# A hybrid state-space and convolution layer: the latent convolution's buffers get rows of 8 KB, and the out-projection's second tile is prepared earlier

## The chip, the cores and the metric

The kernel runs on one core of a Trainium2 chip. The metric is the device time of one execution in microseconds. Before the change it is 1872.1 us, the median of three runs (1870.85 to 1872.3).

## What is computed

One layer over 256 context tokens and 2048 latent tokens (a grid of 32 rows by 64 columns), with a model width of 1024. All tokens are normalised and modulated, and go through one input projection. Its columns feed two branches, whose outputs meet in one output projection. Cut to what matters:

```python
h = rms_norm(x, g_pre) * (1 + scale) + shift
u = h @ w_in
z, xbc, dt_raw, ga, gb, gsil = jnp.split(u, [...], axis=-1)
y_ssd, h_fin = ssd_branch(z, xbc, dt_raw, ...)        # a scan in both directions, gated by silu(z)
c = depthwise_conv(ga * sigmoid(gb), conv_w, conv_b)  # 31 taps along the rows of the grid, per channel
y_conf = silu(layer_norm(c, ln_g, ln_b)) * silu(gsil)
out = jnp.concatenate([y_ssd, y_conf], axis=-1) @ w_out
y = x + gate * rms_norm(out, g_post)
```

For the context the convolution runs along its 256 tokens; for the latent it runs along the 32 grid rows, separately for each of the 64 columns and 1024 channels.

## The kernel before, in words

**Tiling.** The tokens are 18 tiles of 128: tiles 0 and 1 are context, 2 to 17 latent. For the input projection they are grouped in five blocks: block 0 is the context (256 tokens), blocks 1 to 4 are 512 latent tokens each. Channels are handled in groups of 128, numbered j = 0 to 7. Float32 products are made from three matmuls on split operands (high x high, low x high, high x low; lines 391 to 393), so each weight has a high half `wh` and a low half `wl`.

**Phases.** Half 0 projects blocks 1, 2 and 0, half 1 blocks 3 and 4. In each half come the scan's columns (`xp`), then eight `gab_unit`s (the convolution's gated input; matmuls `gb` and `ga`, line 391), then silu units for z and for the gate gsil (`silu_unit`; matmuls `sp`). These units are interleaved with the scan (`px`, `py`, `po`, and its DMAs `yp<-yg`, `st<-sb`), with the context's convolution on DVE (`cg`, line 608), and in half 1 with `lat_conv`, the latent's. `SLOT` says which of the buffers of normalised input each block takes.

**The convolution's path.** `gab_unit` stores its result (`gth`) for channel group j and one block to the DRAM buffer `GL[j]` (line 556): 128 channels, for each one a row of 512 tokens, 2 KB. The latent convolution wants grid rows on the partitions, since the taps run along them. So `lat_load` (line 629) reads `GL[j]` back transposed, into `cx`: four DMAs, each 32 rows x 32 channels x 64 columns, in pieces of 64 columns, 256 B. It also loads the taps (`kd`, line 628). `lat_conv` multiplies 32 x 32 tap matrices with the columns (`cp`, line 648), adds the bias into `cvv` (line 652), and stores it to `CV` (line 657), again in four DMAs of 1024 pieces of 256 B, so that `CV` is channel-major over tokens. Last, `conf_load` (line 1098) reads one tile of 128 tokens, all channels, in 1024 pieces of 512 B.

**Queues.** SP issues nearly all DMAs, one after the other: a DMA whose buffer or data isn't ready holds all behind it, weight loads (`wh<-whd`, `wl<-wld`, lines 359 and 360) among them. A scheduler that keeps a timeline of its own fixes the order on each engine.

**The transition.** The out-projection works tile by tile in the order 17, 16, ..., 0. For a tile it takes the scan's output `y` (with state products `qo`, gate by `z`, sum of squares `zr`), scales it by a norm and splits it into `yh` and `yl`; and the convolution's output `cn` (centred by the mean `cm`, squared into `v`, summed into `nq`, scaled, silu, gated by `gsl`), split into `ph` and `pl`. `norms` sums `zr` and `nq` over the partitions by matmul (`pm`), takes roots on DVE and POOL (`yms`, `yr`), and `spread` hands them to all partitions by matmul (`pn`). The matmuls `op` then multiply both with the out-projection's weights, 16 pairs `woh` and `wol`. `load_wo` (lines 969 to 976) makes a pair: a DMA to a staging tile `wst`, a cast on ACT, a subtraction on DVE. Staging has two buffers in turn. Weights 9 to 15 are loaded only when the last silu unit is done, since their pool takes over memory of that phase. While that goes on, before prepares tile 17's end and tile 16's whole input.

**Line 77.** In the loop, DVE, ACT and PE run through the wrapper `InOrder`: with `on` set, each instruction is kept behind the one that the program issued before it on that engine, so the scheduler can't move it ahead. What was issued before `on` was set, it may still order freely among itself. Loop instructions appear as line 77 in the profile, whichever helper records them.

The wrapper and the loop's head:

```python
        f = getattr(self._eng, name)
        if not self.on:
            return f
        return lambda *a, **k: self._tc.keep_in_program_order(f(*a, **k))
...
    V.on = S.on = T.on = True
    for a, i in enumerate(order):
        banks(i)
        pt = hl(p2, "p", 1, i, v)
        out_part(pso[i], yh, 0, 1)
        rs = None if last else norms(nxt, yz, nq)
```

Of the kernel before, what the change touches and what calls it, by code (L numbers as in the profile page):

```python
# [17 lines left out]
P = 128  # L18
D = 1024
KT = D // P  # L20
# [7 lines left out]
TOK = (0, 256, 768, 1280, 1792)  # L28
BNS = (256, 512, 512, 512, 512)
ORDER = ((1, 2, 0), (3, 4))  # L30
SLOT = (0, 1, 2, 1, 2)
RAWO = (2, 260, 772, 130, 642)
NF = 3
PREP = 16
# [27 lines left out]
def take(gen, n):  # L62
    for _ in range(n):
        yield next(gen, None)
# [16 lines left out]
def backbone_kernel(ctx, tc, xa, xt_in, cols, rows, wconv, conf_b, gp_row, bg_row, state0, w_mod, w_dt, w_in, w_out,  # L81
# [12 lines left out]
    def dram(name, shape):  # L94
        return drp.tile(shape, F32, tag=name, name=name)
# [1 line left out]
    XB = [dram(f"xb{h}", [NCT * P, n]) for h, n in ((0, N1), (1, N2))]  # L97
    HALO = dram("halo", [NCT, P, 130])
    ZS = [dram(f"zs{h}", [D, HT[h] * P]) for h in range(2)]
    GL = [dram(f"gl{j}", [P, NT * P]) for j in range(KT)]  # L100
    GS = [dram(f"gs{h}", [D, HT[h] * P]) for h in range(2)]
    CV = dram("cv", [D, NT * P])
    YP = [dram(f"yp{i}", [P, D]) for i in range(NT)]
    ST = [dram(f"st{i}", [P, D]) for i in range(NT)]
    LT = [dram(f"lt{h}", [HT[h] * 32, P]) for h in range(2)]
# [437 lines left out]
    def gab_unit(half, j, hb):  # L543
        wb = next_w()
        wa = next_w()
        gl_done.discard(j)
        for b in ORDER[half]:
            BN, o = BNS[b], TOK[b]
            pg = bank("mm", f"gb{half}_{j}_{b}")
            yield from mm_cm(pg, wb, hb[b])  # L550
            th = ev(f"gth{half}_{j}_{b}")[:, :BN]
            S.activation(th, pg[:, :BN], AF.Tanh, scale=0.5)
            pa_ = bank("mm", f"ga{half}_{j}_{b}")
            yield from mm_cm(pa_, wa, hb[b])
            V.scalar_tensor_tensor(th, th, 1.0, pa_[:, :BN], ADD, MUL)  # L555
            DMA.dma_start(GL[j][:, o:o + BN], th)
        if half:
            gl_done.add(j)

    def silu_unit(half, c0, dst, j, hb, order=None):  # L560
        w = next_w()
        for b in order or ORDER[half]:
            BN, o = BNS[b], TOK[b] - half * HT[0] * P
            ps = bank("mm", f"sp{half}_{c0}_{j}_{b}")
            yield from mm_cm(ps, w, hb[b])
            th = ev(f"sth{half}_{c0}_{j}_{b}")[:, :BN]
            S.activation(th, ps[:, :BN], AF.Tanh, scale=0.5)  # L567
            V.scalar_tensor_tensor(th, th, 1.0, ps[:, :BN], ADD, MUL)  # L568
            DMA.dma_start(dst[half][j * P:(j + 1) * P, o:o + BN], th)
# [28 lines left out]
    def ctx_conv(j, tile):  # L598
        g = tile(f"cg{j}")
        G.memset(g[:, 0:15], 0.0)  # L600
        G.memset(g[:, 271:286], 0.0)
        DMA.dma_start(g[:, 15:271], GL[j][:, 0:256])
        yield
        acc = g[:, 512:768]
        w0 = C_CONFW + j * CW
        V.tensor_scalar(acc, g[:, 0:256], cv[:, w0:w0 + 1], cfb2[:, j:j + 1], MUL, ADD)
        for t in range(1, CW):
            V.scalar_tensor_tensor(acc, g[:, t:t + 256], cv[:, w0 + t:w0 + t + 1], acc, MUL, ADD)  # L608
            if t % 3 == 0:
                yield  # L610
        o = g[:, 768:1024]
        S.mul(o, acc, 0.5)
        DMA.dma_start(CV[j * P:(j + 1) * P, 0:256], o)
        yield


# [4 lines left out]
    def lat_load(j, lp):  # L621
        kd = lp.tile([P, 32, 32], F32, tag="kd", name=f"kd{j}", bufs=2)
        x = lp.tile([P, 32, 64], F32, tag="cx", name=f"cx{j}", bufs=2)
        lat_in[j] = kd, x
        for a in range(4):
            rs = slice(a * 32, (a + 1) * 32)
            src = bass.AP(tensor=wconv.tensor, offset=(j * 4 + a) * 64 * 32, ap=[[32, 32], [1, 1024]])
            DMA.dma_start(kd[rs].rearrange("p r g -> p (r g)"), src)
            DMA.dma_start(x[rs], GL[j][:, 256:].rearrange("(g a) (r w) -> a r g w", a=4, w=64)[a])

    def lat_conv(j, lp, cbb, more):
        if j not in lat_in:
            lat_load(j, lp)
        kd, x = lat_in.pop(j)
        yield
        kt = lp.tile([P, 32, 32], F32, tag="kt", name=f"kt{j}", bufs=1)
        S.copy(kt[:, :, ::-1].rearrange("p g r -> p r g"), kd)
        if more(j + 1):
            lat_load(j + 1, lp)
        yield  # L640
        vt = lp.tile([P, 32, 64], F32, tag="cvv", name=f"cvv{j}", bufs=1)
        for h in range(2):
            ps = {a: bank("ss", f"cp{j}_{a}") for a in (2 * h, 2 * h + 1)}
            for q in range(8):
                for u in range(4):
                    for a in ps:
                        rs = slice(a * 32, (a + 1) * 32)
                        T.matmul(ps[a][u * 32:(u + 1) * 32, q * 64:(q + 1) * 64], kt[rs, u * 8 + q, :], x[rs, u * 8 + q, :],
                                 start=True, stop=True)
            yield  # L650
            for a in ps:
                V.scalar_tensor_tensor(vt[:, a::4, :], ps[a].rearrange("p (c w) -> p c w", w=64), 0.5,
                                       cbb[:, j, a::4].unsqueeze(2).to_broadcast([P, 8, 64]), MUL, ADD)
            yield
        for u in range(4):
            c0 = j * P + u * 32
            DMA.dma_start(CV[c0:c0 + 32, 256:].rearrange("c (r w) -> r c w", w=64), vt[u * 32:(u + 1) * 32])


    def pass_a(i):  # L660
# [217 lines left out]
    def run(gen):  # L878
        for _ in gen:
            pass  # L880
# [36 lines left out]
    xbc_phase(0, first, hb, [hprep(2, hb), hprep(0, hb)], tails, dt_post(0))  # L917
    extra = chain([gate_rows()] + [ctx_conv(j, big) for j in range(4)])
    interleave(post(0, 6), merge(scan(range(9)), 68, extra, 9 + 4 * 13), 90 * 8)
    last = [silu_unit(0, GS0, GS, j, hb, (1, 2, 0)) for j in (6, 7)]  # L920
    prep = hprep(3, hb)
    s = 0
    for b in range(3):
# [99 lines left out]
    def state_add(i):  # L1023
        for g in range(2):
            sg = sl[i]["st"][:, g * 512:(g + 1) * 512]
            if i == NCTX - 1:
                V.tensor_copy(Sb[g], sg)
            else:
                V.tensor_tensor(Sb[g], Sb[g], sg, ADD)
# [49 lines left out]
    def lo(t):  # L1079
        V.tensor_tensor(t[1], t[2], t[0].bitcast(F32), SUB)  # L1080
# [14 lines left out]

    def conf_load(i):
        n = p2.tile([P, 8, P], F32, tag="cn", name=f"cn{i}", bufs=2)
        DMA.dma_start(n, CV[:, i * P:(i + 1) * P].rearrange("(c p) t -> p c t", p=P))
        return n

    def conf_sum(i, n):
        v = p2.tile([P, 8, P], F32, tag="v", name=f"v{i}", bufs=2)
        return v, sum8(v[:, 0, :], v[:, 0:4, :], n)

    def conf_mean(i, t):
        mean = bank("ss", f"cm{i}")[:, 0:P]
        T.matmul(mean, ones, t, start=True, stop=True)
        return mean

    def conf_centre(n, mean):  # L1110
        V.scalar_tensor_tensor(n, rows8(mean), -1.0 / D, n, MUL, ADD)

    def conf_square(v, n):
        S.activation(v, n, AF.Square)
        return v

    def conf_sqsum(i, v):
        return v, sum8(p2.tile([P, P], F32, tag="nq", name=f"nq{i}", bufs=1), v[:, 0:4, :], v)

    def gs_load(i):  # L1120
        gs = p2.tile([P, 8, P], F32, tag="gs", name=f"gsl{i}", bufs=1)
        DMA.dma_start(gs, chan_slice(GS, i))
        return gs

    def conf_scale(n, pb):
        V.tensor_tensor(n, n, rows8(pb[:, P:2 * P]), MUL)
# [63 lines left out]
    for g in range(2):  # L1190
        state_decay(i, g)
    state_add(i)
    run(take(blocks, 5))
    for k in range(6, 9):
        load_wo(k, wo2)
        run(take(blocks, 8))
    run(blocks)
    last = [silu_unit(1, GS0, GS, j, hb) for j in range(5, 8)]
    for b in range(2):
        for m, u in enumerate(last):  # L1200
            run(take(u, 8))
            if b == 0 and m == 1:
                rs = norms(i, yz, None)
            if b == 1 and m == 0:
                ssd_scale(i, yz[0], spread(i, rs))
                yh = hl(p0, "y", 2, i, yz[0])
                lo(yh)
                ph_b[1].close()
                p2 = ph_1.enter_context(tc.tile_pool(name="p2", bufs=1))
                n = conf_load(i)  # L1210
                v, t = conf_sum(i, n)
                conf_centre(n, conf_mean(i, t))
    for u in last:
        run(u)
    v, nq = conf_sqsum(i, conf_square(v, n))
    conf_scale(n, spread(i, norms(i, None, (v, nq))))
    gs = gs_load(i)
    conf_silu(n, v)
    conf_gate(v, gs)
    ph_b[2].close()  # L1220
    ph_h.close()
    p3 = ph_1.enter_context(tc.tile_pool(name="p3", bufs=1))
# [1 line left out]
    for k in range(9, 16):  # L1224
        load_wo(k, wo4)
    load_gg(0)
    i = order[1]
    ssd_load(i)
    st_load(i)
    n = conf_load(i)  # L1230
    state_mm(i)
    y_state(i)
    y_gate(i)
    yz = y_sum(i)
    for g in range(2):
        state_decay(i, g)
    v2, t = conf_sum(i, n)
    conf_centre(n, conf_mean(i, t))
    nq = conf_sqsum(i, conf_square(v2, n))
    gs = gs_load(i)  # L1240
    ssd_load(order[2])
    n2 = conf_load(order[2])
    V.on = S.on = T.on = True
# [133 lines left out]
```

## Time and profile before

| what | value |
|---|---|
| median of three runs | 1872.1 us |
| the profiled execution | 1872.28 us |
| its span in the trace | 1870.5 us |
| mean granted TensorE clock | 0.984 |
| PE, DVE, ACT busy | 97%, 64%, 46% |
| DMA moved | 375.22 MB, mean 201 GB/s |
| half-0 gab units, roughly | 230 to 560 us |
| half-1 gab units and latent convolution, roughly | 930 to 1230 us |
| last silu units end | 1405 us |
| out-projection loop | to the end |

How to read it: engine names are PE (matmul), PEld (its weight loads), DVE, ACT, POOL and SP (its queue as SPq). `out<-in` gives an instruction's output and input by the program's names. A bracket at the end of a timeline's row is the idle time ahead of that instruction and what ended it. In the table of windows each row is one stretch: its length, then busy time and count for PE, PEld, DVE, ACT and POOL, then the granted PE clock as a share of full speed, the DMA engines' busy share and GB/s.

### The profile page before, as it was taken

How to read it: one execution, taken by the hardware profiler on the slowest of the kernel's cores; microseconds unless marked ns; L12 is line 12 of the kernel's file. 1: busy time of each engine (PE TensorE's matmuls, PEld its weight loads, DVE VectorE, ACT ScalarE, POOL GpSimd, SP SyncE). 2: the span in 40 equal slices, each digit the busy share in tenths (PEclk: the TensorE clock that was granted, in tenths of full speed). 3: DMA queues.
4: the chain of work that ended last, by engine and by line, in shares of the span. 5: the costliest groups of instructions: out<-in, count | busy, mean ns of one | idle time of the engine just before them, and what ended most of it. 6: DMA issues, size and time to landing. Idle time of an engine off the chain costs nothing.

```text
span 1870.5 us, 30012 instructions
## 1 busy us (share of the span) xinstructions
PE 1808.1 (97%) x11223; PEld 1493.1 (80%) x11223; DVE 1203.1 (64%) x1841; ACT 863.8 (46%) x1956; POOL 175.9 (9%) x281
## 2 busy tenths in 40 slices
PE   7899999999999999999998989999997999999998
PEld 4788887788888888888876767777886888888887
DVE  2477887785555553577587845666347777777773
ACT  3646424455445441644224545553326454444441
POOL 0002001111101100100001111110000111111110
PEclk9899999999999999999999999999998999999999
DMA  8656575576566654545589798895967656666632
GB/s 298 219 199 210 203 241 181 175 254 219 195 217 211 226 196 169 167 155 189 170 200 233 199 251 229 258 244 175 331 189 209 183 167 174 172 171 178 182 106 79
DMA packets 305309, 375.22 MB, mean 201 GB/s; under 512 B 85254, under 2 KB 204678, under 8 KB 305164
## 3 DMA queue, kind: packets, MB, share of 16 engines
q1 hardware_dynamic: 284428, 335.56, 58.1%
q10 hardware_dynamic: 20736, 37.76, 7.1%
q8 instruction: 88, 1.44, 0.3%
q14 instruction: 57, 0.47, 0.1%
HBM read 243.66 MB, written 129.59 MB: 200 GB/s over the span
## 4 chain that ended last, share of the span: by engine, by line
PE 85%; DMA 7%; DVE 4%; ACT 1%; issue 1%; SPq 1%; POOL 0%; POOLq 0%; DVEq 0%; ACTq 0%
PE op L77 21%; PE sp L391 7%; PE sp L392 7%; PE sp L393 7%; PE xp L391 5%; PE xp L392 5%; PE xp L393 5%; PE ga L391 3%; PE ga L393 2%; PE ga L392 2%; PE gb L391 2%; PE gb L393 2%; PE gb L392 2%; DMA lb<-lt 2%; PE py L732 2%; DVE cg L608 2%
## 5 line engine op out<-in xcount | busy, mean ns | idle before, releaser
L696 ACT ACTIVATE lb<-lb,WB 128x128 f32<-128x128 f32 x576 | 184.3, 391 | 167.7 <-POOL lb L688 162.1
L391 PE MATMUL sp<-hh,wh 128*128 128x512 f32 (+1 forms) x640 | 238.5, 373 | 0.0
L392 PE MATMUL sp<-hl,wh 128*128 128x512 f32 (+1 forms) x640 | 236.0, 369 | 0.0
L393 PE MATMUL sp<-hh,wl 128*128 128x512 f32 (+1 forms) x640 | 235.8, 368 | 0.0
L391 PE MATMUL xp<-hh,wh 128*128 128x512 f32 (+1 forms) x480 | 179.3, 375 | 6.1 <-ACT wh L366 4.9
L688 POOL TENSOR_SCALAR_AFFINE_SELECT lb<-lb 128x512 f32<-128x512 f32 x144 | 112.6, 786 | 714.2 <-ACT el L685 366.7
L393 PE MATMUL xp<-hh,wl 128*128 128x512 f32 (+1 forms) x480 | 179.0, 373 | 0.0
L392 PE MATMUL xp<-hl,wh 128*128 128x512 f32 (+1 forms) x480 | 178.9, 373 | 0.0
L488 DVE SCALAR_TENSOR_TENSOR cva<-raw,cwh,cva 128x1280 f32<-128x1280 f32 (+1 forms) x96 | 142.1, 1488 | 19.7 <-ACT cva L482 17.9
L391 PEld LDWEIGHTS sp<-hh,wh 128*128 128x128 f32 x640 | 120.6, 189 | 20.8 <-DVE sth L568 0.4
L393 PEld LDWEIGHTS sp<-hh,wl 128*128 128x128 f32 x640 | 120.6, 188 | 20.7
L392 PEld LDWEIGHTS sp<-hl,wh 128*128 128x128 f32 x640 | 120.7, 189 | 19.8
L391 PE MATMUL ga<-hh,wh 128*128 128x512 f32 (+1 forms) x320 | 122.0, 381 | 6.8 <-DMA wh<-whd 6.3
L391 PE MATMUL gb<-hh,wh 128*128 128x512 f32 (+1 forms) x320 | 121.4, 379 | 5.3 <-DVE gth L555 5.3
L393 PE MATMUL ga<-hh,wl 128*128 128x512 f32 (+1 forms) x320 | 119.4, 373 | 0.5 <-DMA wl<-wld 0.5
L392 PE MATMUL gb<-hl,wh 128*128 128x512 f32 (+1 forms) x320 | 119.6, 374 | 0.0
L393 PE MATMUL gb<-hh,wl 128*128 128x512 f32 (+1 forms) x320 | 119.6, 374 | 0.0
L392 PE MATMUL ga<-hl,wh 128*128 128x512 f32 (+1 forms) x320 | 119.2, 373 | 0.0
L568 DVE SCALAR_TENSOR_TENSOR sth<-sth,sp 128x512 f32<-128x512 f32 (+1 forms) x80 | 50.4, 630 | 97.3 <-ACT sth L567 96.9
L391 PEld LDWEIGHTS xp<-hh,wh 128*128 128x128 f32 x480 | 92.1, 192 | 23.2 <-ACT wh L366 5.5
L608 DVE SCALAR_TENSOR_TENSOR cg<-cg,cv 128x256 f32<-128x256 f32 x240 | 107.6, 487 | 0.6
L392 PEld LDWEIGHTS xp<-hl,wh 128*128 128x128 f32 x480 | 91.7, 191 | 15.7 <-DVE hl L312 0.4
(252 smaller groups left out, 3745.8 us busy)
## 6 DMA issues: line engine op xcount, KB each, us to landing
lb<-lt ACTq DMA_DIRECT2D x144, 256.0 KB, 4.5
wr<-in_w_in SPq DMA_DIRECT2D x88, 256.0 KB, 4.7
whd<-wh SPq DMA_DIRECT2D x44, 512.0 KB, 3.6
wld<-wl SPq DMA_DIRECT2D x44, 512.0 KB, 5.2
wh<-whd SPq DMA_DIRECT2D x44, 512.0 KB, 4.6
wl<-wld SPq DMA_DIRECT2D x44, 512.0 KB, 5.8
xT<-xb SPq DMA_DIRECT2D x18, 512.0 KB, 5.0
yp<-yg SPq DMA_DIRECT2D x36, 256.0 KB, 4.3
```

Of the source, the lines that this page charges most:

```text
L77: return lambda *a, **k: self._tc.keep_in_program_order(f(*a, **k))
L391: T.matmul(ps[:, :BN], wh[:, k, :], hh[:, k, :], start=(k == 0), stop=False)
L392: T.matmul(ps[:, :BN], wh[:, k, :], hl[:, k, :], start=False, stop=False)
L393: T.matmul(ps[:, :BN], wl[:, k, :], hh[:, k, :], start=False, stop=(k == KT - 1))
L488: V.scalar_tensor_tensor(a[:, :n], raw[:, t:t + n], cwh[:, ct * 5 + t:ct * 5 + t + 1], a[:, :n], MUL, ADD)
L568: V.scalar_tensor_tensor(th, th, 1.0, ps[:, :BN], ADD, MUL)
L608: V.scalar_tensor_tensor(acc, g[:, t:t + 256], cv[:, w0 + t:w0 + t + 1], acc, MUL, ADD)
L688: G.affine_select(E[g, hq, d], E[g, hq, d], pattern=[[0, 4], [sg, P]], compare_op=ALU.is_ge, fill=NEG, base=0, channel_multiplier=-sg)
L696: S.activation(lb[:, h, :], lb[:, h, :], AF.Exp, bias=WB[:, i, c + h:c + h + 1])
L732: T.matmul(py[g][j * HD:(j + 1) * HD, q * P:(q + 1) * P], xt[g][:, h * HD:(h + 1) * HD], E[g, hq, 0][:, t, :], start=True, stop=True)
```

## The change

**Rows of 8 KB.** `GL` is split. `GLC[j]` holds the context; `GLX[j]` holds the latent's 128 x 2048 in the layout that `cx` has in memory, so `lat_load` reads it with a single DMA of 128 rows of 8 KB. The transposition moves to `gab_unit`: each store of a latent block becomes four DMAs of 32 x 8 pieces of 64 columns (256 B). `CV` is split too: `CVC` for the context, `CVL` for the latent with grid rows outermost. `lat_conv` stores 32 rows of 8 KB per DMA, still four DMAs. `conf_load` of a latent tile is now two DMAs, one for each of its two grid rows, of 1024 pieces of 256 B.

**Order of the gate's blocks.** The last silu units of half 1 take block 4 ahead of block 3, those of half 0 take 2, 1, 0; `SLOT` is changed to fit.

**The second tile.** The loads and all preparation of tile 16 (`ssd_load`, `st_load`, `state_mm`, `y_state`, `y_gate`, `y_sum`, `state_decay`, `conf_load`, `conf_sum`, `conf_centre`, `conf_square`, `conf_sqsum`), and tile 17's scale, silu and gate, move from behind the loop over `load_wo(9)` to `load_wo(15)`, or from just ahead of it, into the last silu units.

```diff
-SLOT = (0, 1, 2, 1, 2)
+SLOT = (0, 1, 2, 2, 1)
...
             V.scalar_tensor_tensor(th, th, 1.0, pa_[:, :BN], ADD, MUL)
-            DMA.dma_start(GL[j][:, o:o + BN], th)
+            if b == 0:
+                DMA.dma_start(GLC[j], th)
+                continue
+            r0 = (o - NCTX * P) // 64
+            for a in range(4):
+                DMA.dma_start(GLX[j][a * 32 + r0:a * 32 + r0 + BN // 64, :].rearrange("r (g w) -> g r w", w=64),
+                              th.rearrange("(g a) (r w) -> a g r w", a=4, w=64)[a])
...
-            DMA.dma_start(x[rs], GL[j][:, 256:].rearrange("(g a) (r w) -> a r g w", a=4, w=64)[a])
+        DMA.dma_start(x.rearrange("p g w -> p (g w)"), GLX[j])
...
-            c0 = j * P + u * 32
-            DMA.dma_start(CV[c0:c0 + 32, 256:].rearrange("c (r w) -> r c w", w=64), vt[u * 32:(u + 1) * 32])
+            DMA.dma_start(CVL[j * 32:(j + 1) * 32, u * 2048:(u + 1) * 2048],
+                          vt[u * 32:(u + 1) * 32].rearrange("r c w -> r (c w)"))
...
-        DMA.dma_start(n, CV[:, i * P:(i + 1) * P].rearrange("(c p) t -> p c t", p=P))
+        if i < NCTX:
+            DMA.dma_start(n, CVC[:, i * P:(i + 1) * P].rearrange("(c p) t -> p c t", p=P))
+        else:
+            for e in range(2):
+                DMA.dma_start(n[:, :, e * 64:(e + 1) * 64],
+                              CVL.rearrange("(j r) (p w) -> r p j w", r=32, w=64)[2 * (i - NCTX) + e])
...
     state_add(i)
+    i1 = order[1]
+    ssd_load(i1)
+    st_load(i1)
...
-    last = [silu_unit(1, GS0, GS, j, hb) for j in range(5, 8)]
+    last = [silu_unit(1, GS0, GS, j, hb, (4, 3)) for j in range(5, 8)]
     for b in range(2):
         for m, u in enumerate(last):
             run(take(u, 8))
             if b == 0 and m == 1:
                 rs = norms(i, yz, None)
-            if b == 1 and m == 0:
+                state_mm(i1)
+                y_state(i1)
+                y_gate(i1)
+            if b == 0 and m == 2:
                 ssd_scale(i, yz[0], spread(i, rs))
                 yh = hl(p0, "y", 2, i, yz[0])
                 lo(yh)
+                yz = y_sum(i1)
+                for g in range(2):
+                    state_decay(i1, g)
...
-                n = conf_load(i)
-                v, t = conf_sum(i, n)
-                conf_centre(n, conf_mean(i, t))
+                nn = [conf_load(i), conf_load(i1)]
+                vv = [conf_sum(j, n) for j, n in zip((i, i1), nn)]
+                for (v, t), j, n in zip(vv, (i, i1), nn):
+                    conf_centre(n, conf_mean(j, t))
+                    conf_square(v, n)
+                nq = conf_sqsum(i, vv[0][0])
+            if b == 1 and m == 0:
+                rs = norms(i, None, nq)
+                nq = conf_sqsum(i1, vv[1][0])
+            if b == 1 and m == 1:
+                n, v = nn[0], vv[0][0]
+                conf_scale(n, spread(i, rs))
+                conf_silu(n, v)
+            if b == 1 and m == 2:
+                gs = gs_load(i)
+                conf_gate(v, gs)
+                n = nn[1]
+                gs = gs_load(i1)
     for u in last:
         run(u)
-    v, nq = conf_sqsum(i, conf_square(v, n))
-    conf_scale(n, spread(i, norms(i, None, (v, nq))))
-    gs = gs_load(i)
-    conf_silu(n, v)
-    conf_gate(v, gs)
...
     for k in range(9, 16):
         load_wo(k, wo4)
     load_gg(0)
-    i = order[1]
-    ssd_load(i)
-    st_load(i)
-    n = conf_load(i)
...
-    gs = gs_load(i)
     ssd_load(order[2])
     n2 = conf_load(order[2])
     V.on = S.on = T.on = True
```

More of the change, by code (lines that the diff above doesn't have):

```diff
@@ L99, in backbone_kernel @@
     ZS = [dram(f"zs{h}", [D, HT[h] * P]) for h in range(2)]
-    GL = [dram(f"gl{j}", [P, NT * P]) for j in range(KT)]
+    GLC = [dram(f"glc{j}", [P, NCTX * P]) for j in range(KT)]
+    GLX = [dram(f"glx{j}", [P, LAT]) for j in range(KT)]
     GS = [dram(f"gs{h}", [D, HT[h] * P]) for h in range(2)]
-    CV = dram("cv", [D, NT * P])
+    CVC = dram("cvc", [D, NCTX * P])
+    CVL = dram("cvl", [KT * 32, P * 64])
     YP = [dram(f"yp{i}", [P, D]) for i in range(NT)]
@@ L601, in ctx_conv @@
         G.memset(g[:, 271:286], 0.0)
-        DMA.dma_start(g[:, 15:271], GL[j][:, 0:256])
+        DMA.dma_start(g[:, 15:271], GLC[j])
         yield
@@ L612, in ctx_conv @@
         S.mul(o, acc, 0.5)
-        DMA.dma_start(CV[j * P:(j + 1) * P, 0:256], o)
+        DMA.dma_start(CVC[j * P:(j + 1) * P, :], o)
         yield
@@ L919, in backbone_kernel @@
     interleave(post(0, 6), merge(scan(range(9)), 68, extra, 9 + 4 * 13), 90 * 8)
-    last = [silu_unit(0, GS0, GS, j, hb, (1, 2, 0)) for j in (6, 7)]
+    last = [silu_unit(0, GS0, GS, j, hb, (2, 1, 0)) for j in (6, 7)]
     prep = hprep(3, hb)
@@ L1226, in backbone_kernel @@
     load_gg(0)
-    i = order[1]
-    ssd_load(i)
-    st_load(i)
-    n = conf_load(i)
[L1231 to L1239, printed above, removed]
-    gs = gs_load(i)
     ssd_load(order[2])
```

## The prediction

> **What bounds the kernel now.** I read the page first, then the windows, then PE's waits, then the timelines of SP and DVE where PE waits. The page says whose idle time counts:
>
> ```profile
> span 1870.5 us, 30012 instructions
> PE 1808.1 (97%) x11223; PEld 1493.1 (80%) x11223; DVE 1203.1 (64%) x1841; ACT 863.8 (46%) x1956; POOL 175.9 (9%) x281
> ```
>
> PE is busy 97%. The change adds and takes away no PE work, so it can only move PE's idle time and the clock's loss behind it. The windows show where that sits (first columns: length, PE busy; near the end PEclk, DMA share):
>
> ```profile
> 230.00:560.00 330.00, 323.69 (x1810) 269.32 (x1809) 226.48 (x391) 149.43 (x364) 37.41 (x56) 0.99 0.62 209
> 930.00:1000.00 70.00, 67.13 (x570) 53.78 (x568) 52.72 (x106) 22.37 (x46) 4.11 (x7) 0.98 0.95 206
> 1000.00:1100.00 100.00, 84.56 (x890) 65.53 (x888) 73.02 (x136) 48.38 (x124) 14.92 (x20) 0.93 0.88 233
> 1100.00:1190.00 90.00, 90.00 (x965) 71.24 (x964) 51.27 (x80) 46.83 (x119) 13.19 (x18) 1.00 0.92 243
> 1440.00:1870.00 430.00, 423.88 (x2057) 356.05 (x2055) 301.85 (x454) 199.84 (x510) 43.94 (x50) 1.00 0.57 158
> ```
>
> Two places matter. In the latent convolution's stage, 930 to 1100, PE idles 2.9 + 15.4 = 18.3 us and loses 0.02 x 67.1 + 0.07 x 84.6 = 7.2 us to the clock: 25.5 us. PE's waits (total us, times, longest) name the causes, and the second place, one wait of 12.3 us at the transition to the out-projection (line 77):
>
> ```profile
> PE pm L77 <- DVE zr L986: 12.3, 1, 12.3
> PE ga L391 <- DMA wh<-whd: 6.3, 2, 5.5
> PE px L708 <- issue: 4.1, 2, 2.7
> PE cp L648 <- DVE yg L773: 3.8, 1, 3.8
> PE cp L648 <- DVE cvv L652: 1.5, 2, 1.1
> ```
>
> **Part 1, the convolution's rows: a gain.** SP's timeline shows why wh and yg came late:
>
> ```profile
> 1017.16 4.27 SPq L629 DMA_DIRECT2D cx<-gl  x4
> 1021.48 1.49 SPq L776 DMA_DIRECT2D yp<-yg  x1
> 1075.61 5.01 SPq L657 DMA_DIRECT2D cv<-cvv  x4
> 1084.18 0.38 SPq L359 DMA_DIRECT2D wh<-whd  x1
> 1092.24 0.76 PE L391 MATMUL ga<-hh,wh 128*128 128x512 f32 x1 [5.47 <-DMA wh<-whd]
> L629 SPq DMA_DIRECT2D cx<-gl x32: 319/800/3232, 947.3 to 1228.9; - x32
> L657 SPq DMA_DIRECT2D cv<-cvv x32: 318/1252/3841, 974.5 to 1307.3; - x32
> ```
>
> Four small-piece stores of cv hold SP for 5.0 us; the weight load behind them is issued at 1084.18 and PE waits for it until 1092.24. Likewise the yp store goes out only after four cx loads of 4.27 us; DVE waits for that store, and PE for DVE (3.8). At their medians (second figure, ns) the two kinds of issue cost SP 32 x 0.80 + 32 x 1.25 = 66 us. Now there are 8 cx issues and 32 cv issues of 8 KB rows, and 48 more glx stores in this half. The smallest issue in the rows is 0.32; by it these are 88 x 0.32 = 28 us. The glx stores are small pieces too, a quarter as many as a cv store has; were each 0.8, the sum is 40 x 0.32 + 48 x 0.8 = 51. SP is freed of 15 to 38 us. Of pieces, 2 x 32 x 1024 of 256 B go and 64 x 256 come in this stage. One place on SP, the conv stage's fifth j, before and after:
>
> ```order
> L556 DMA gl_72<-gth_4_3_9736 128x512
> L628 DMA kd_10813<-in_wconv 32x1024 x2
> L657 DMA cv<-cvv_9778 32x32x64 x4
> L665 DMA bc_10330<-xb_64 128x4x128
> L628 DMA kd_10813<-in_wconv 32x1024 x2
> L359 DMA wh_1_9664<-whd_137 128x1024
> ```
> ```order
> L563 DMA glx_80<-gth_4_3_9805 32x8x64 x4
> L636 DMA kd_10894<-in_wconv 32x1024
> L664 DMA cvl<-cvv_9847 32x2048 x4
> L636 DMA kd_10894<-in_wconv 32x1024 x3
> L673 DMA bc_10408<-xb_64 128x4x128
> L361 DMA wh_1_9736<-whd_146 128x1024
> ```
>
> The order hardly moved; the shapes did. This is the very place at which PE then waited 5.5 us, and the clock stayed low after it:
>
> ```profile
> 1092.00:1097.00 5.00, 4.76 (x11) 3.39 (x12) 1.98 (x3) 2.03 (x7) 0.08 (x1) 0.50 1.00 383
> 1097.00:1100.00 3.00, 3.00 (x12) 2.36 (x10) 0.00 (x0) 0.00 (x0) 0.00 (x0) 0.77 1.06 298
> ```
>
> That stall costs 5.5 + 0.5 x 5 + 0.23 x 3 = 8.7 us; with yg 3.8 and cvv 1.5 this is 14.0, and half of the other clock loss, (7.2 - 3.2)/2 = 2.0: 16. px's 4.1 us "issue" has no releaser that I can tie to SP; I add a quarter. Gain **17 us**, between 7 (new waits fill half of the traced 14) and the whole 25.5.
>
> **Part 2, pieces moved elsewhere: about 1 us lost.** In half 0, 48 more glx issues at 0.32 to 0.8 are 15 to 38 us of SP time over 330 us in which PE is idle 6.3; cover is that weights are loaded ahead. I take +1, from 0 to +4. In the out-projection a tile's cn load becomes two of 256 B pieces. It has cover (the last rows, from the list of DMA issues: KB, median us from issue to landing):
>
> ```profile
> 1459.81 0.36 SPq L1098 DMA_DIRECT2D cn<-cv  x1
> 1476.77 0.68 DVE L77 TENSOR_TENSOR v<-cn 128x512 f32<-128x512 f32 x1
> cn<-cv SPq DMA_DIRECT2D x18, 512.0 KB, 5.4
> gl<-gth SPq DMA_DIRECT2D x32, 256.0 KB, 2.9
> gs<-sth SPq DMA_DIRECT2D x32, 256.0 KB, 4.4
> cx<-gl SPq DMA_DIRECT2D x32, 256.0 KB, 5.5
> cv<-cvv SPq DMA_DIRECT2D x32, 256.0 KB, 5.4
> ```
>
> It is used 17.0 us after its issue and lands in 5.4. Small-piece cx loads land 256 KB in 5.5, so 512 KB at worst in 11: still 6 us early. Cost 0; without that cover it would be 16 x 5.6 = 90 us.
>
> **Part 3, the transition: a loss.** It is meant to take away pm's 12.3 us wait for tile 16's zr. Its work (sums, gate, squares) now stands before the last silu units' end. But line 77 pins each loop instruction behind the previous one traced on its engine. Before, that was tile 16's square and sum, ahead of most weight conversions, so the loop could slip between them. Now it is the last conversion, load_wo(15). DVE at the transition, before and then after (wol: low half of out-projection weights 9 to 15; yms: the loop's first DVE step, the norm of tile 16):
>
> ```order
> L976 TENSOR_TENSOR wol_13705<-wst_13707,woh_13706 128x1024
> L976 TENSOR_TENSOR wol_13711<-wst_13713,woh_13712 128x1024
> L984 TENSOR_TENSOR v_13797<-v_13797 128x512
> L984 TENSOR_TENSOR z_13756<-z_13756 128x512
> L985 TENSOR_TENSOR v_13797<-v_13797 128x256
> L985 TENSOR_TENSOR z_13756<-z_13756 128x256
> L986 TENSOR_TENSOR nq_13805<-v_13797 128x128
> L986 TENSOR_TENSOR zr_13777<-z_13756 128x128
> L976 TENSOR_TENSOR wol_13717<-wst_13719,woh_13718 128x1024
> L77 TENSOR_SCALAR yms_13836<-pm_13833 128x1
> ```
> ```order
> L1147 SCALAR_TENSOR_TENSOR v_13696<-v_13696,gsl_13824 128x1024
> L984 TENSOR_TENSOR wol_13850<-wst_13852,woh_13851 128x1024
> L984 TENSOR_TENSOR wol_13856<-wst_13858,woh_13857 128x1024
> L984 TENSOR_TENSOR wol_13862<-wst_13864,woh_13863 128x1024
> L984 TENSOR_TENSOR wol_13868<-wst_13870,woh_13869 128x1024
> L984 TENSOR_TENSOR wol_13874<-wst_13876,woh_13875 128x1024
> L984 TENSOR_TENSOR wol_13880<-wst_13882,woh_13881 128x1024
> L984 TENSOR_TENSOR wol_13886<-wst_13888,woh_13887 128x1024
> L77 TENSOR_SCALAR yms_13920<-pm_13917 128x1
> ```
>
> Three conversions stood before yms, now all seven. And PE, in its own order, needs tile 16's pn (two steps behind yms) after 24 out-projection matmuls. Times of before:
>
> ```profile
> 1404.44 0.39 PE L392 MATMUL sp<-hl,wh 128*128 128x512 f32 x1
> 1404.67 0.39 PE L393 MATMUL sp<-hh,wl 128*128 128x512 f32 x1
> 1406.06 0.49 PE L1070 MATMUL pn<-ident,yr 128*128 128x128 f32 x2 [0.88 <-POOL yr L148]
> 1406.38 1.95 PE L1014 MATMUL qo<-ct,Sb 128*128 128x128 f32 x16
> 1422.20 0.56 PE L77 MATMUL pm<-ones,zr 128*128 128x1 f32 x2 [12.26 <-DVE zr L986]
> 1423.05 1.20 PE L77 MATMUL op<-woh,yh 128*128 128x512 f32 x2
> 1428.66 0.61 PE L77 MATMUL pn<-ident,yr 128*128 128x128 f32 x4
> 1406.44 0.32 SPq L569 DMA_DIRECT2D gs<-sth  x1
> 1410.62 3.18 ACT L1130 ACTIVATE v<-cn,cv 128x128 f32<-128x128 f32 x8
> 1417.42 2.36 DVE L976 TENSOR_TENSOR wol<-wst,woh 128x1024 fp32r<-128x1024 f32 x2
> 1425.95 0.21 DVE L77 TENSOR_SCALAR yms<-pm 128x1 f32<-128x1 f32 x2
> 1436.79 1.23 DVE L976 TENSOR_TENSOR wol<-wst,woh 128x1024 fp32r<-128x1024 f32 x1 [0.18 <-ACT woh L975]
> ```
>
> Let T0 be the end of the last silu unit, 1404.67 + 0.23 = 1404.9 in before (matmuls start 0.23 apart): tile 16's pn stood at T0 + 23.8. After, tile 17's pn comes at T0 + 1.5 (1.2 in before, and one op matmul), its scale (1.2) and silu (3.2 and a start) done by T0 + 6.2. Its gate no longer waits for its gs load, as block 4 is now stored first. The first cast on ACT waits for the silu and for the last gs store, whose buffers its weights take over; that store was issued 1.5 after T0 and the median lands 4.4 later, in crowded stretches 5: T0 + 6.7. A cast takes about 1.0, so wol 9 starts at T0 + 7.9. The wol stretch took 1436.79 + 1.23 - 1417.42 = 20.6 us, and DVE's seven of 1.23 are 8.6 of them: the pace is set by the two staging buffers, whose next load SP may issue only when the subtract before has freed one. The change leaves that round of load, cast and subtract as it is. So it ends at T0 + 28.5; yms to pn took 1428.66 - 1425.95 = 2.7: pn at **T0 + 31.2**, 7.4 later. The 16 qo matmuls (2.0) move ahead of T0 and push it back. Behind the stall the 18 op matmuls took 5.6 us where PE's pace, 0.23 each, gives 4.1, and pm took 0.85 for about 0.25: 2.1 of slow clock, which now falls behind pn. Sum +7.4 + 2.0 + 2.1 = **+11.5**, from +7 (that stretch a fifth shorter, since SP now issues its loads back to back, with z and stl no longer between them) to +16 (the last gs store or a staging load later by one landing of 4.4). The four cn loads of tiles 17 and 16 stand on SP ahead of staging loads 10 and 9, the y load and three gs stores. They are four issues where two were; I cost them at nothing, as those two conversions start only after the silu. If they land late, T0 itself moves: that too is in the upper end.
>
> **Sum.** Against the profiled execution, 1872.28 (span 1870.5 + 1.8), which is 0.2 above the median: 1872.3 - 17 + 1 + 11.5 = 1867.8; against the median **1867.6**.
>
> **Rivals.** (a) *Slower:* the glx stores take back what SP gains, and the transition's loss is left. At 256 KB each, small-piece stores of cv land in 5.4 where gl's 2 KB rows take 2.9. A cx load must wait on SP for the last glx store of its j: 2.5 longer, eight times, is 20 us of SP's hold, more than the low end of what it is freed of (15), and wh stands behind. For it: new glx stores stand right ahead of wh, as cv's did. Against it: in 1100 to 1190 the DMA share is 0.92 and PE never stalls, so weights come in time when SP isn't held in one piece. With a gain of 4 left: 1872.1 - 4 + 1 + 11.5 = 1880.6; it decides once under 8.8 of the 25.5 us go. The Trainium skill (DMA: Bandwidth & Descriptors, section Specifications) has a rule on (a)'s side: under 512 B a transfer misses full rate, with a read-modify-write. By it the estimate for a 256 B store is about twice the time; the two landings, 5.4 to 2.9, agree, though no trace here shows the mechanism. (b) *The transition works as meant:* pm's wait goes and none comes, 12.3 + 2.1 less: 1872.1 - 17 + 1 - 14.4 = 1841.7. The order of DVE speaks against it; it needs the conversions to end about when yh's matmuls do. A half-way case, the conversions starting 5 us earlier and with rounds shorter by 4 in all, leaves +2.5 here: 1858.6. (c) *Nothing measurable:* a gain of 12.5 pays for the transition: 1872.1. Nothing speaks against it but the size of the traced waits. That the change doesn't do what it says is excluded by the orders.
>
> **How the numbers follow.** Forecast (gain 13 to 25 with the transition's loss, 1860 to 1871) 0.50; (c), 1871 to 1875, 0.18; (a) 0.20; (b) 0.04 and its half-way case 0.08. Two of ten left out: **1854 to 1881**. A difference below 0.2%, 3.7 us, can't be told from none. Faster than 1868.4: (b) 0.04, half-way 0.08 and 0.38 of the forecast's 0.50, thus 0.50; the forecast's other 0.12, (c) and a little of (a) make 0.31; slower than 1875.8: 0.19.
>
> **What would show it.** Right: cx and cv issues near 0.35 us, the ga wait for wh gone, PE over 90 us busy in the 100 us of the gab stage; at the transition one wait of PE pn for POOL yr of about 24 us (31.2 less 7 of matmuls), with yms directly behind the seventh wol. Wrong: if that wait is under 15 us, part 3 falls, and if PE's idle time in the stage stays over 12 us, part 1.

## The result and the profile after

The changed kernel takes 1902.07 us (median of four runs, 1897.5 to 1903.85) where before takes 1872.2 (the median of four runs, one more than in the table ahead): ratio 1.0155, 95% interval 1.0133 to 1.0177. I had forecast 1867.6, in a range of 1854 to 1881. It is slower, and by more than any of my cases. The profiled execution took 1897.5 us, its span is 1895.8, which is 25.3 longer than before's.

First PE's waits again, in the changed kernel (total us, times, longest):

```profile
PE pn L77 <- POOL yr L150: 24.0, 1, 24.0
PE px L716 <- issue: 11.7, 3, 5.3
...
PE px L716 <- DVE cvv L660: 4.9, 1, 4.9
...
PE po L747 <- issue: 3.7, 1, 3.7
PE cp L656 <- issue: 3.0, 1, 3.0
```

The first row is the forecast wait at the transition. The `ga` wait for `wh` is gone, as forecast too. But the scan's matmuls (`px`, `po`) and the convolution's (`cp`) now wait for 23 us in the rows shown, where in before they waited for 10 (4.1 + 3.8 + 1.5 + 1.0). The windows of the convolution stage:

```profile
930.00:1000.00 70.00, 67.17 (x586) 54.23 (x585) 55.57 (x113) 26.96 (x61) 6.38 (x11) 1.00 0.81 228
1000.00:1100.00 100.00, 87.37 (x917) 67.93 (x915) 73.04 (x135) 44.28 (x110) 15.11 (x17) 0.95 0.70 215
1100.00:1190.00 90.00, 80.64 (x878) 63.97 (x877) 44.93 (x71) 44.26 (x112) 11.21 (x16) 0.94 0.73 223
1190.00:1330.00 140.00, 135.08 (x1427) 106.99 (x1426) 80.20 (x126) 64.11 (x155) 13.97 (x20) 0.98 0.67 207
```

Up to 1100 PE is busy 3 us more than before. From 1100 to 1330, where before had no idle time at all, it idles 9.4 + 4.9 us and the clock dips to 0.94. PE's idle time adds up to 15.5 us before 1100 and to 29.7 before 1330; over 12 us was to be the sign that part 1 is wrong. The DMA share fell in every window, from 0.88 to 0.70 between 1000 and 1100: the DMAs did get lighter, and it bought nothing. SP's own issue times came out near the forecast 0.35 us for the wide rows, and between my two figures, 0.32 and 0.8, for the small ones (minimum, median, maximum in ns):

```profile
L637 SPq DMA_DIRECT2D cx<-glx x8: 319/350/569, 946.6 to 1227.0; - x8
...
L664 SPq DMA_DIRECT2D cvl<-cvv x32: 308/422/2092, 972.0 to 1321.5; - x32
...
L563 SPq DMA_DIRECT2D glx<-gth x128: 576/607/2346, 245.5 to 1195.8; - x128
```

Where the 25.3 us of span lie, by PE's first and last matmuls of a kind (`xp` ends the columns of half 1's scan, `sp` the silu units, `op` the out-projection):

| stretch | before | after | difference |
|---|---|---|---|
| span's start to the first xp | 36.7 | 37.9 | +1.2 |
| first xp to last xp (half 0 lies in it) | 876.6 | 875.0 | -1.6 |
| last xp to last sp (convolution stage) | 491.3 | 507.5 | +16.2, of which 2.0 are the qo matmuls moved in |
| last sp to last op (transition, out-projection) | 457.9 | 467.4 | +9.5, or +11.5 with the moved 2.0 |

So the transition lost 11.5 us, the sum that I had worked out. What failed is the stage: 14.2 lost instead of 17 gained.

The transition's timeline on DVE shows the seven conversions ahead of `yms`:

```profile
1428.35 1.22 DVE L1147 SCALAR_TENSOR_TENSOR v<-v,gsl 128x1024 f32<-128x1024 f32 x1 [4.60 <-ACT v L1143]
1429.49 2.35 DVE L984 TENSOR_TENSOR wol<-wst,woh 128x1024 fp32r<-128x1024 f32 x2
...
1449.27 1.23 DVE L984 TENSOR_TENSOR wol<-wst,woh 128x1024 fp32r<-128x1024 f32 x1 [2.82 <-ACT woh L983]
1450.41 0.22 DVE L77 TENSOR_SCALAR yms<-pm 128x1 f32<-128x1 f32 x2
```

With T0 = 1420.6, wol 9 starts at T0 + 8.9 (I had 7.9), the stretch takes 21.0 (20.6), and pn starts at T0 + 31.6 (31.2).

### The profile page after: what moved, and what is told of

The parts are those of the page before. It is cut to its first block, busy times and chain, and to the rows that moved or that the text cites. A ratio compares the mean times of both kernels' runs of the same rounds, so it can differ in the third digit from the quotient of the medians.

```text
span 1895.8 us, 30131 instructions
## 1 busy us (share of the span) xinstructions
PE 1808.4 (95%) x11223; PEld 1494.4 (79%) x11223; DVE 1202.5 (63%) x1841; ACT 865.5 (46%) x1956; POOL 182.6 (10%) x281
## 4 chain that ended last, share of the span: by engine, by line
PE 70%; DMA 16%; DVE 5%; ACT 3%; issue 2%; POOL 2%; SPq 1%; ACTq 0%; POOLq 0%; DVEq 0%
PE op L77 21%; DMA lb<-lt 8%; PE sp L393 6%; PE sp L394 6%; PE sp L395 6%; PE xp L393 5%; PE xp L394 5%; PE xp L395 5%; DMA xin<-in_xa 2%; POOL lb L696 2%; ACT lb L704 2%; DVE cg L616 2%; PE qo L77 1%; DMA yp<-yg 1%; DMA wr<-in_w_in 1%
## 5 line engine op out<-in xcount | busy, mean ns | idle before, releaser
L696 POOL TENSOR_SCALAR_AFFINE_SELECT lb<-lb 128x512 f32<-128x512 f32 x144 | 118.9, 829 | 734.6 <-ACT el L693 370.3
L490 DVE SCALAR_TENSOR_TENSOR cva<-raw,cwh,cva 128x1280 f32<-128x1280 f32 (+1 forms) x96 | 141.9, 1486 | 17.6 <-ACT cva L484 15.8
L708 DVE TENSOR_TENSOR lb<-lb,lb 128x512 f32<-128x512 f32 x72 | 50.2, 697 | 97.2 <-ACT lb L704 75.5
```

The costliest lines, as they stand in the source:

```text
L490: V.scalar_tensor_tensor(a[:, :n], raw[:, t:t + n], cwh[:, ct * 5 + t:ct * 5 + t + 1], a[:, :n], MUL, ADD)
L696: G.affine_select(E[g, hq, d], E[g, hq, d], pattern=[[0, 4], [sg, P]], compare_op=ALU.is_ge, fill=NEG, base=0, channel_multiplier=-sg)
L708: V.tensor_tensor(a, a, E[g, hq, 1], ADD)
```

## What a stall of the stage looks like

The stage is shared by the scan, whose chain runs through all engines. For each step ACT's own queue loads a tile of decays (`lb<-lt`, line 684), POOL masks it (line 696), ACT takes exponentials of it (`el` line 693, `lb` line 704), DVE combines them (line 708), PE multiplies (`py`), DVE sums into `yg` and SP stores it (`yp`). Here is one of the new stalls of `px`, the rows of four engines in order of time; the first fence is ACT:

```profile
1099.82 0.33 ACTq L684 DMA_DIRECT2D lb<-lt  x1
...
1105.37 0.84 ACT L693 ACTIVATE el<-lb 64x256 f32<-64x256 f32 x2 [3.83 <-DMA lb<-lt]
1106.95 1.28 ACT L704 ACTIVATE lb<-lb,WB 128x128 f32<-128x128 f32 x4 [0.74 <-POOL lb L696]
```

DVE, SP and PE behind it:

```profile
1108.32 0.69 DVE L708 TENSOR_TENSOR lb<-lb,lb 128x512 f32<-128x512 f32 x1 [5.33 <-ACT lb L704]
...
1109.64 0.69 DVE L783 TENSOR_TENSOR yg<-yg,yo 128x512 f32<-128x512 f32 x1
...
1114.92 1.10 DVE L776 TENSOR_TENSOR yg<-xT,dcol 128x512 f32<-128x512 f32 x1 [3.68 <-DMA yp<-yg]
1115.94 0.68 DVE L759 TENSOR_TENSOR Sf<-Sf,eTf 128x512 f32<-128x512 f32 x1
1116.54 0.68 DVE L761 TENSOR_TENSOR yo<-po,el 128x512 f32<-128x512 f32 x1
```

```profile
1099.98 2.71 SPq L563 DMA_DIRECT2D glx<-gth  x4
1110.36 0.33 SPq L784 DMA_DIRECT2D yp<-yg  x1
```

```profile
1117.32 0.87 PE L716 MATMUL px<-ident,xT 128*128 128x128 f32 x4 [4.30 <-issue]
```

ACT issues a decay load and, after only four more instructions, stands 3.8 us waiting for it. DVE waits 5.3 for ACT; `yg` is therefore late, its store goes out at 1110.36, and the next `yg` waits for that store. In DVE's fixed order `yo` stands behind it and ends at 1117.22. `px` starts 0.10 later. That `yo` frees the bank of matmul output memory (PSUM) which `px` takes is inferred from this 0.10; the profile names no releaser. SP's small-piece stores hold nothing back here: the four `glx` are issued by 1102.69, and SP's next DMA is the `yp` store, which goes out as soon as `yg` is ready.

The waits of ACT for decay loads, within 915 to 1330, before and after:

```profile
ACT el L685 <- DMA lb<-lt: 19.7, 9, 4.4
```

```profile
ACT el L693 <- DMA lb<-lt: 44.1, 17, 5.5
```

The loads themselves take no longer (median from issue to landing over the program 4.5 us before, 4.2 after). What changed is where the scheduler placed them. The edit of the buffers touches no ACT instruction. Yet of ACT's 546 rows between the last xp and the last sp, 283 stand in another place in the two orders that the experiments below replay (that of before, and that of before with both buffers changed). Between a decay load of half 1 and the first ACT instruction that uses it stand, in the median of 72 loads, 7 other ACT instructions before and 5 after; 4 or fewer stand there 23 times before, 35 times after.

The theory, then: *the stage's loss is not the DMAs' doing; the scheduler, whose timeline saw other DMAs, re-ordered engines that the change doesn't touch, and the scan's chain pays for it.* The rival is my own (a): the new small-piece stores cost SP, and what queues behind SP, more than the wide rows save.

## The experiments

"Ratio" is against before on the same chip, with its 95% interval. "Stage" is last xp to last sp in the profiled execution, as in the table above; "ACT's wait" is the row just shown.

### Each part alone

transition_only keeps the buffers of before and takes the rest of the change. The diff is against the changed kernel.

```diff
-    GLC = [dram(f"glc{j}", [P, NCTX * P]) for j in range(KT)]
-    GLX = [dram(f"glx{j}", [P, LAT]) for j in range(KT)]
+    GL = [dram(f"gl{j}", [P, NT * P]) for j in range(KT)]
...
-    CVC = dram("cvc", [D, NCTX * P])
-    CVL = dram("cvl", [KT * 32, P * 64])
+    CV = dram("cv", [D, NT * P])
...
```

> The buffers of before (GL and CV in their old layout), with the new block order and the new transition. Theory A (the two losses are separate: the pinned loop costs 11.5 us at the transition, and the convolution stage loses 14 us because of the new layout): about 1884 us, PE waits 24 us at tile 16's pn, and the convolution stage keeps the idle time of before, 18 us between 930 and 1330. Theory B (the stage loses because of the new order of blocks or of tile 16's early loads): about 1898, with about 30 us of idle time in the stage.

1887.2 us, ratio 1.0062 (1.0041 to 1.0084). Its stage takes 491.6 us with the 2.0 of qo matmuls in it (before: 491.3), and pn waits 24.3. Theory A: the transition by itself costs what was summed, and costs the stage nothing. PE is busy 382.9 us between 930 and 1330, in before 381.7. In this kernel PE, ACT and DVE stand in the stage row for row as in before, up to the steps that the change moves in at its end.

cv_only and gl_only take one buffer each, with before's transition.

```diff
-            c0 = j * P + u * 32
-            DMA.dma_start(CV[c0:c0 + 32, 256:].rearrange("c (r w) -> r c w", w=64), vt[u * 32:(u + 1) * 32])
+            DMA.dma_start(CVL[j * 32:(j + 1) * 32, u * 2048:(u + 1) * 2048],
+                          vt[u * 32:(u + 1) * 32].rearrange("r c w -> r (c w)"))
...
```

> Before, with the convolution's output alone in the new layout (8 KB rows stored, 256 B pieces loaded by the out-projection). Theory A1 (the small-piece stores of cv held SP, and freeing it pays as I had predicted): the 5.5 us wait for wh goes, 1860 to 1866 us. Theory A2 (the scan's own chain of decay loads, masks and exponentials sets the stage's pace, so PE meets the scan's next step earlier and waits there instead): 1869 to 1875, with a longer wait of px.

1890.81 us, ratio 1.0085 (1.0057 to 1.0113): outside both expectations, and on the wrong side. This edit has no small-piece store in it, only wide rows in their place, and its stage still lost 15.8 us (507.1). PE still waits for `wh` once, for 4.2 us. That speaks against the rival (a).

```diff
-            DMA.dma_start(GL[j][:, o:o + BN], th)
+            if b == 0:
+                DMA.dma_start(GLC[j], th)
+                continue
+            r0 = (o - NCTX * P) // 64
+            for a in range(4):
+                DMA.dma_start(GLX[j][a * 32 + r0:a * 32 + r0 + BN // 64, :].rearrange("r (g w) -> g r w", w=64),
+                              th.rearrange("(g a) (r w) -> a g r w", a=4, w=64)[a])
...
```

> Before, with the convolution's input alone in the new layout (four stores of 256 B pieces for each block, one load of 8 KB rows). Theory A1 (the 48 extra small-piece stores of this half, 0.6 us each on SP, delay the scan's stores and loads): 1880 to 1888 us, more than the output's part. Theory A2 (the scan's own chain sets the pace, SP matters little): 1869 to 1876.

1882.69 us, ratio 1.0044 (1.0029 to 1.0059); stage 497.4. It fits A1 by its number; but cv_only, which A1 would have faster, is worse than this one. Two edits of opposite kinds both lose: neither piece size nor SP's time sorts them. In both, ACT's wait had grown, from 19.7 to 44.4 (cv_only) and 37.2 (gl_only).

### The same order, other DMAs

inorder_old and inorder_new switch the wrapper of line 77 on in the stage, without and with the new layouts. ACT, PE and DVE then stand in the program's order in both, row for row.

```diff
     run(take(blocks, 24))
+    V.on = S.on = T.on = True
     interleave(take(blocks, 24), [sc_] * 4, 24)
...
     run(extra)
+    V.on = S.on = T.on = False
```

> Before, with the wrapper of line 77 switched on through the convolution stage of half 1, so that PE, ACT (its decay loads too) and DVE keep the order of the program there. A base for the next kernel alone; program order knows no waiting times, so I expect 1885 to 1940 us.

1915.35 us, ratio 1.0218 (1.0194 to 1.0242).

> The same, with both buffers in the new layout: the order on PE, ACT and DVE in the stage is then the same, row for row, and only the DMAs differ. Theory P (the stage of the changed kernel lost its 14 us because the scheduler, which plans by its own estimates of the DMAs, put ACT and DVE into another order; the new DMAs by themselves are no worse): the same time as the old layout in program order, or up to 15 us less. Theory D (the new DMAs cost: 0.6 us for each small-piece glx store on SP, and whatever queues behind): 8 to 20 us more than the old layout in program order.

1919.57 us, ratio 1.0243 (1.0219 to 1.0267). The intervals overlap, though all four runs are above the four of the old layouts. The stage takes 532.6 us against 534.8 with the old layouts; in the profiled executions the longer part is ahead of it, where the order isn't held (first xp to last xp 881.1 against 877.5). At equal order the new DMAs neither cost the stage 14 us nor give it 17.

both_layouts is the base of the next kernels: before with both buffers changed, planned anew. The two behind it hold PE, ACT and DVE to a recorded order, those of the next section one engine. A table (not shown) lists, for each engine, in which order a scheduler's earlier plan put the traced instructions; each is made to follow the one before it in the table. SP is planned anew.

```diff
+    for eng, steps in table.items():
+        seq, at, prev = traced[eng], 0, None
...
+        for s in steps:
+            at += s
+            if prev is not None:
+                tc.add_manual_dep(seq[at], prev.name, kind, reason="replay")
+            prev = seq[at]
```

> Before with both buffers in the new layout, and its own transition and block order; the scheduler plans it anew, and its order in the convolution stage is that of the changed kernel. Both theories: the changed kernel less the transition's 12 us, about 1886 to 1891 us.

1892.42 us, ratio 1.0108 (1.0082 to 1.0135), a little above the expectation; stage 507.1, ACT's wait 43.0.

> The same program as both_layouts, but PE, ACT and DVE are held by explicit order to the order that the scheduler made for before, row for row over the whole program; only the DMAs on SP are planned anew. Theory P (the loss of the stage comes from the new order on ACT and DVE, the new DMAs are no worse): 1866 to 1877 us, and the stage's idle time no more than 18 us. Theory D (the new DMAs cost it): 1884 to 1892, as both_layouts.

1875.45 us, ratio 1.0012 (0.9993 to 1.0030), stage 491.5, ACT's wait 25.4. In the trace PE, ACT and DVE run their instructions in before's order. Theory P: with the old order the same DMAs cost nothing that the interval can show.

> The converse: the layouts of before, with PE, ACT and DVE held to the order that the scheduler made for both_layouts. Theory P: slow although no DMA is changed, 1882 to 1895 us. Theory D: the time of before, 1870 to 1877.

1903.01 us, ratio 1.0166 (1.0136 to 1.0197), stage 517.6, ACT's wait 37.1. All the DMAs of before, and slower by 30 us, 8 more than Theory P allowed for. Theory P again, and one thing more: in this order the kernel with the new layouts is 10.6 us faster than that with the old (1892.42 against 1903.01). SP's order differs between the two as well, so that this is the layouts' doing alone is not shown. The rows of ACT's wait, for layout_old_order, both_layouts and old_layout_new_order:

```profile
ACT el L757 <- DMA lb<-lt: 25.4, 11, 5.0
```

```profile
ACT el L693 <- DMA lb<-lt: 43.0, 17, 4.6
```

```profile
ACT el L749 <- DMA lb<-lt: 37.1, 15, 4.4
```

### Which engine's order

> Both buffers in the new layout, ACT alone held to the order that the scheduler made for before; PE and DVE are planned anew around it. If ACT's order makes the loss (it issues the decay loads, and a load that is issued later or waited for earlier delays the whole scan): 1873 to 1880 us. If it is DVE's: 1886 to 1895.

1875.72 us, ratio 1.0003 (0.9984 to 1.0021), stage 489.8. DVE's order stays another one here (in 151 of its 494 places in the stage stands another kind of instruction than in before), and ACT's wait is:

```profile
ACT el L735 <- DMA lb<-lt: 22.8, 9, 5.1
```

> The same with DVE alone held to the old order. If DVE's order makes the loss: 1873 to 1880 us; if ACT's: 1886 to 1895.

1896.91 us, ratio 1.0115 (1.0086 to 1.0143), stage 510.8, and ACT's wait:

```profile
ACT el L736 <- DMA lb<-lt: 45.8, 20, 6.0
```

> The same with PE alone held to the old order, from which the new one differs in a few places only. I expect no help: 1886 to 1895 us. If PE's few places make the loss, 1873 to 1880.

1889.7 us, ratio 1.0078 (1.0051 to 1.0105), stage 499.8, ACT's wait 46.2. Holding ACT alone brings back the whole stage, although PE and DVE are planned anew there; holding DVE alone brings back none of it. PE's is not clear: the ratio is 0.3% below that of both_layouts, with overlapping intervals, and its profiled stage was 7.3 us shorter. It is ACT's order that the loss hangs on.

### The transition

after_unpinned moves two steps of tile 17 behind the conversions, so that they, and not the last conversion, are what the loop is pinned behind.

```diff
-                conf_silu(n, v)
...
-                conf_gate(v, gs)
...
     for k in range(9, 16):
         load_wo(k, wo4)
+    conf_silu(n, v)
+    conf_gate(v, gs)
```

> The changed kernel, with tile 17's silu and gate issued behind the seven weight conversions, so that the loop's instructions are pinned behind these two and not behind the last conversion. Theory A (the pinning makes the 24 us wait): yms stands ahead of the first conversion, the wait at pn falls to about 4 us, 1882 to 1887 us. Rival (the wait is for the weights themselves or for DMA traffic of the transition): the wait moves to an op matmul that needs weight 11 to 15, and the time stays within 5 us of 1902.

1894.01 us, ratio 1.0090 (1.0071 to 1.0110), where the changed kernel had 1.0155: some 12 us less. In the profiled executions last sp to last op takes 456.8 us against 467.4. The 24.0 us wait fell to 3.1 and 0.6, but a new one came behind it, `pm` for tile 15's `zr`:

```profile
PE pm L77 <- DVE zr L77: 5.8, 1, 5.8
...
PE pn L77 <- POOL yr L150: 3.7, 2, 3.1
```

The pinning made the wait, but the gain is 11 or 12 us, where I expected 15 to 20. That the conversions, later on DVE, now delay the tile after is a reading that no run tests.

> The old layouts with the new transition, tile 17's silu and gate issued behind the seven weight conversions. The order of the convolution stage is that of before, row for row. If the two losses are separate, the stage costs nothing here, and the transition is as in the unpinned changed kernel: about 12 us less than the new transition with the pinning, 1872 to 1877 us on a chip where before takes 1872 to 1875. Rival (the layouts gave the unpinned kernel part of its gain): 1880 or more.

1868.34 us, ratio 0.9974 (0.9959 to 0.9989): faster than before, and faster than expected. The stage takes 491.8. At the transition the main waits are 2.1 (pn) and 2.3 (op for a late weight), and last sp to last op takes 451.3. DVE's timeline there:

```profile
1411.66 1.23 DVE L1134 SCALAR_TENSOR_TENSOR v<-v,gsl 128x1024 f32<-128x1024 f32 x1 [4.60 <-ACT v L1130]
1412.80 0.22 DVE L77 TENSOR_SCALAR yms<-pm 128x1 f32<-128x1 f32 x2
1413.71 2.36 DVE L976 TENSOR_TENSOR wol<-wst,woh 128x1024 fp32r<-128x1024 f32 x2 [0.69 <-ACT woh L975]
```

`yms` stands right behind the gate, where the changed kernel had seven conversions between.

staging_four gives the conversions two more buffers:

```diff
-        wr = p0.tile([P, D], F32, tag=("yh", "yl")[k % 2], name=f"wst{k}", bufs=2)
+        if k in (11, 12, 15):
+            wr = p3.tile([P, D], F32, tag="o", name=f"wst{k}", bufs=2)
+        else:
+            wr = p0.tile(..., bufs=2)
```

> The kernel above, with two more staging buffers for weights 9 to 15 (the output tiles of the loop's last step, which are free then): weights 11, 12 and 15 go through them. If the pace of the conversions is set by the two staging buffers, the seventh subtraction ends about 10 us earlier, tile 15's wait for zr (5.8 us in the unpinned kernel) goes, and the time falls by 4 to 9 us: 1864 to 1871. Rival (DMA bandwidth or DVE sets that pace): no change, within 2 us of the kernel above.

1868.71 us, ratio 0.9971 (0.9952 to 0.9990): no change. The seventh subtraction does end early, and the step shows in DVE's timeline:

```profile
1412.82 4.63 DVE L979 TENSOR_TENSOR wol<-wst,woh 128x1024 fp32r<-128x1024 f32 x4 [0.66 <-ACT woh L978]
...
1421.44 2.36 DVE L979 TENSOR_TENSOR wol<-wst,woh 128x1024 fp32r<-128x1024 f32 x2
```

All seven are done at 1423.8; in the kernel above the last one ends at 1437.3. But the 5.8 us wait that I meant to remove belonged to the unpinned kernel with the new layouts, and wasn't there any more. The buffers did set the pace of the conversions. The 2.3 us wait for a late weight went with that, and another took its place, which had been 0.4 in the kernel above:

```profile
PE qo L77 <- DVE Sb L77: 3.4, 1, 3.4
```

Last, the whole change with both repairs: the new layouts, the new transition unpinned, and transition_free's order.

> The changed kernel with tile 17's silu and gate behind the weight conversions, and PE, ACT and DVE held to the order that the scheduler made for the same program in the old layouts (transition_free, 1868 us). Theory P: the layouts cost nothing and the transition's gain is kept, 1858 to 1871 us, faster than before. Theory D: about 1880 to 1890.

1866.78 us, ratio 0.9970 (0.9958 to 0.9983). Faster than before by 0.3%, and not to be told from transition_free. The layouts cost nothing and give nothing that these intervals can show; the transition's gain is kept.

## Why the prediction was wrong

**The transition (part 3) was right**, mechanism and size: the order showed the seven conversions ahead of `yms`, and +11.5 was forecast and measured; the wait of about 24 us came as 24.0. transition_only repeats it alone (24.3). That the sum met to the tenth is luck: the conversions began 1.0 later than forecast and ran 0.4 longer, and `pn` stood 1.8 behind the start of `yms` instead of 2.7.

**Half 0 and the out-projection (part 2) hold.** First xp to last xp took 875.0 us against 876.6, and in the other kernels 874.4 to 881.1 without pattern, so my +1 can't be told from none. `cn`'s small pieces are hidden as argued: in cv_only last sp to last op takes 458.4 us, in before 457.9.

**Part 1 failed, in two steps.** The first is the sentence "The order hardly moved; the shapes did", written on six rows of SP. I compared SP there, and DVE at the transition, but not ACT in the stage, which the change doesn't mention. With ACT's old order the loss is gone (old_act_order, 1.0003), with the new order it comes even without the DMAs (old_layout_new_order, 1.0166). What I forecast as a change of shapes was, in time, a change of plan: 14.2 us lost in the stage.

The second step is the gain itself: "Four small-piece stores of cv hold SP for 5.0 us", therefore freeing SP gives 17. In layout_old_order PE, ACT and DVE stand in before's order and the `wh` wait is gone. SP is freed of 14 us on the three kinds of issue that I had summed (`cx`, `cv` and `glx` against `gl`, 913 to 1330: 68.0 us where before has 82.2), just under my 15 to 38. But the stage takes 491.5 us against 491.3. PE's waits there, 915 to 1410:

```profile
PE cp L720 <- ACT sb L833: 3.9, 1, 3.9
PE px L780 <- issue: 3.6, 2, 2.0
PE pst L817 <- issue: 2.9, 1, 2.9
PE cp L720 <- DVE yg L845: 2.3, 1, 2.3
PE pst L817 <- DVE cvv L724: 1.9, 1, 1.9
```

The term of 17 us measured nothing: between 930 and 1330 PE idles 17.7 us, in before 18.3. The waits moved to other steps of the scan (`px`, `pst`) and of the convolution (`cp`). I had priced each wait of PE as if its end were the only limit. That the scan's chain of load, mask, exponential and store stood just behind fits these rows, and px's 4.1 us "issue" may have been a sign of it; I had added a quarter of it to the gain.

**Rival (a) had the sign and not the cause.** Its `glx` stores do cost 0.61 us each on SP (median), but cv_only, which has none, loses more than gl_only. No rival of mine had an engine re-ordered that the diff leaves alone, so the range, made of gains and losses by DMAs, ended at 1881.

**What stays open.** Why the scheduler's timeline moved ACT so is not measured; that it took the loads as landing sooner than they do is a guess. Nor is it shown which of ACT's moved rows make the loss. The wait for decay loads grew in every kernel in which a new plan made the stage longer, but it isn't the measure of it: old_layout_new_order waits less than both_layouts (37.1 against 43.0) and its stage is longer (517.6 against 507.1). The split by part isn't a sum either: stages of 507.1, 497.4 and, for both, 507.1.

## What to carry to other kernels

Where a scheduler plans all engines on one timeline, an edit of a DMA's shape can re-order engines it doesn't name: compare the order of every engine in every stage before pricing anything. Then separate plan from hardware by holding the order fixed and changing the DMAs, and the converse. And when a wait goes, ask which chain arrives next: in this stage, in which several engines take turns, taking a wait of 5.5 us away gave nothing back.

## What the runs showed of the hardware

Lighter DMA traffic alone gave no time: in the stage (930 to 1330) the DMA share fell from 0.85 in before to 0.74 in layout_old_order, at PE busy times of 381.7 and 382.3 us. Pieces of 256 B did no harm in the out-projection, where other work covers them (last sp to last op 458.4 us in cv_only, 457.9 in before). Stores of 256 KB landed in 5.4 us (median) in 256 B pieces, before's `cv`, and in 4.2 in rows of 8 KB, `cvl` of the changed kernel (4.7 in layout_old_order). The Trainium skill (DMA: Bandwidth & Descriptors, section Specifications) sets the least transfer for full rate at 512 B; the two landings agree with that in direction, and in time it cost nothing that layout_old_order (1.0012) could show. The out-projection's `cn` loads landed in 3.8 us for 256 KB in 256 B pieces and in 5.4 for 512 KB in 512 B pieces, which doesn't compare the pieces alone, since the size differs too. On SP a DMA of 256 such pieces took a median of 0.61 us to issue and one of 32 rows of 8 KB 0.42; the minimum was 0.58 for the one and 0.31 for the other.
